# Seven pairs of up-projection tiles by one step of Strassen's scheme, in a hybrid decoder block on one core

## The chip, the cores and the metric

The kernel runs on one core of a Trainium2 chip. It computes one layer of a decoder for one sequence of 512 tokens, with 16 learned meta tokens ahead of them. The metric is the time of one execution on the device in microseconds (us). Five engines work side by side, each through its own queue in order: PE multiplies matrices (PEld is its weight load), DVE does elementwise work on one or two tensors, ACT does elementwise functions of one tensor, POOL is used here for little, and SP issues transfers from the main memory.

## The reference, cut to what matters

The layer normalises its input, projects it, mixes tokens in two ways, adds a projection of the mixed values, and ends in a gated part of which this is the whole:

```python
def rmsnorm(x, w):
    xf = x.astype(jnp.float32)
    y = xf * lax.rsqrt(jnp.mean(xf * xf, axis=-1, keepdims=True) + EPS)
    return (y * w.astype(jnp.float32)).astype(x.dtype)

def causal_dwconv(x, w, b):
    k_taps, length = w.shape[0], x.shape[1]
    xp = jnp.pad(x, ((0, 0), (k_taps - 1, 0), (0, 0)))
    y = b + xp[:, 0:length] * w[0]
    for k in range(1, k_taps):
        y = y + xp[:, k:k + length] * w[k]
    return y

def conv_glu_ffn(h, w_up, conv_w, conv_b, w_down):
    u = causal_dwconv(h @ w_up, conv_w, conv_b)
    gate, val = jnp.split(u, 2, axis=-1)
    return (jax.nn.silu(gate) * val) @ w_down
...
        h = h + conv_glu_ffn(rmsnorm(h, norm2_w[l]), ffn_w_up[l], ffn_conv_w[l],
                             ffn_conv_b[l], ffn_w_down[l])
    y = rmsnorm(h, final_norm_w)
    return y[:, N_META:, :]
```

The model is 1024 wide, the gated part 2816: `w_up` has 2 x 2816 columns, 22 tiles of 128 for the gate and 22 for the value. The convolution has three taps.

## The kernel before, in words

Channels lie on the 128 partitions, tokens along the free axis. A weight tile is 128 output channels by 1024 inputs (8 blocks k of 128). Every product in float32 quality is made of three faster ones: a weight tile `raw` is split into `whi` (ACT, L160) and `wlo` = raw - whi (DVE, L161), the tokens likewise into hi and lo, and for each k PE does whi x hi, whi x lo and wlo x hi. `product` (L190) does this for two halves of the tokens, which lie in two banks of PE's result memory: 8 x 3 x 2 = 48 matmuls for a tile, of 258 and 256 columns in the gated part.

The program runs in stages: input projection with both mixers (tiles `pj`), output projection (`pout`), the gated part's up-projection (`pup`), its down-projection (`pdn`), and a last normalisation. In the up stage pair j is the gate tile `pupj` and the value tile `pup(22+j)`: tile 24 is the value tile of pair 2. `conv3` (L790 and on) makes a tile: the product of `u2h`, `u2l` (tokens times the norm's weight, not yet divided by their size), then on DVE `fr` = pup x rstd2 (L797), which divides, on ACT the tap of the newest token with the bias (`fc`, L799), and on DVE two more taps (L801). After both tiles ACT does the silu, DVE the product (L810), and ACT and DVE split it into `ac_hi` and `ac_lo` (L813, L814) for the down stage. The reciprocal root `rstd2` exists only after the first tile, from `psn` (L785) through ACT (L130, L131).

Nothing of the order is written by hand. A scheduler puts the instructions of each engine in one list ahead of time, by priorities: weights come first (`first`), reading results out of PE's memory can be put higher still (`evac`). On the chip each engine follows its list and waits where an operand is not there or a buffer is not free. Buffers rotate: `pj` has two buffers of two banks for the tiles, `px` four of one bank, `raw`, `whi` and `wlo` three each, `pr` (for `fr` and `fc`) four. `weights` (L178 and on) asks for tiles two ahead, so a transfer into `raw` starts when the split of the tile three before it is done.

Of the kernel before, what the change touches and what calls it, by code (L numbers as in the profile page):

```python
# [29 lines left out]
O = 512 - HALF  # L30
# [24 lines left out]
def tile_block(ctx: ExitStack, tc: tile.TileContext, xT, w_in, w_dt, w_out, w_up, w_down,  # L55
               par, consts, consti, out, dbg=None):
    nc = tc.nc
    V, A, G, PE = nc.vector, nc.scalar, nc.gpsimd, nc.tensor

    cp = ctx.enter_context(tc.tile_pool(name="cp", bufs=1))  # L60
    wp = ctx.enter_context(tc.tile_pool(name="wp", bufs=3))
# [18 lines left out]
    def banks2(name):  # L80
        return pj.tile([P, 1024], F32, tag="pj", name=name)
# [13 lines left out]
    pt = cp.tile([P, C_ALL], F32, name="pt")  # L95
# [3 lines left out]
    def col(c):  # L99
        return pt[:, c:c + 1]  # L100
# [6 lines left out]
    with first(300000):  # L107
        w = A.activation(warm[:], eps[:], AF.Copy)
# [32 lines left out]
    chunks = [(("in", j), w_in[j], KD) for j in order]  # L141
# [9 lines left out]
    wnext = [0]  # L151

    def raw_tiles(key):
        name = "_".join(map(str, key))
        return (wp.tile([P, KD * P], F32, tag="raw", name=f"raw_{name}", bufs=3),
                wp.tile([P, KD * P], F32R, tag="whi", name=f"whi_{name}"),
                wp.tile([P, KD * P], F32R, tag="wlo", name=f"wlo_{name}"))

    def split_weights(raw, hi, lo, d, eng):
        A.activation(hi[:, d], raw[:, d], AF.Copy)  # L160
        eng.tensor_tensor(lo[:, d], raw[:, d], hi[:, d].bitcast(F32), ALU.subtract)  # L161

    def ahead(n):
        while wnext[0] < min(n, len(chunks)):
            key, src, kc = chunks[wnext[0]]
            with first():
# [9 lines left out]
    def weights(*key):  # L176
        used[0] += 1
        ahead(used[0] + 2)  # L178
        return wdone.pop(key)

    def product(groups, xh, xl, t0, nk, k0=0):


        for k in range(len(xh)):
            first, last = k0 + k == 0, k0 + k == nk - 1
            for ps, (hi, lo) in groups:
                wh, wl = hi[:, k * P:(k + 1) * P], lo[:, k * P:(k + 1) * P]
                for w, x, s, e in ((wh, xh[k], first, False), (wh, xl[k], False, False), (wl, xh[k], False, last)):
                    for a0, a1 in ((t0, HALF), (HALF, NT)):
                        PE.matmul(ps[:, O + a0:O + a1], w, x[:, a0:a1], start=s, stop=e)  # L190

    vh, vl, xt, sqs = [], [], [], []
    starts = [raw_tiles(("in", j)) for j in (BT, CT)]
    wnext[0] = 2
    with first(200000):
        for k in range(0, KD, 2):
            d = slice(k * P, (k + 2) * P)
            for j, w, kx in ((BT, starts[0], k), (CT, starts[1], k + 1)):  # L200
                t = slot(f"x{kx}", tag="y")
# [8 lines left out]
        for k in range(KD):  # L210
# [3 lines left out]
            tag = "b0" if k < 4 else "b1"  # L214
            hi, lo = slot(f"v{k}_hi", dtype=F32R, tag=tag), slot(f"v{k}_lo", dtype=F32R, tag=tag)
# [75 lines left out]
    for n, (a0, a1) in enumerate(((0, HALF), (HALF, NT))):  # L291
        p = bank(f"psd{n}")[0:66, :]
# [444 lines left out]
    for h in range(NH):  # L737
        o = os_[h]
        ps = proj(GT + h, T0)
        sg = slot(f"sg{h}", tag="pr")  # L740
# [3 lines left out]
        hi, lo = slot(f"oa{h}_hi", dtype=F32R), slot(f"oa{h}_lo", dtype=F32R)  # L744
# [7 lines left out]
    hs, u2h, u2l = [], [], []  # L752
    pos = {}
    acc = None
    for j, s in oorder:
        w = weights("out", j, s)
# [10 lines left out]
        hi, lo = slot(f"u2h{j}", dtype=F32R, tag="u"), slot(f"u2l{j}", dtype=F32R, tag="u")  # L767
# [22 lines left out]
    def conv3(j):  # L790
        w = weights("up", j)
        ps = banks2(f"pup{j}")
        product([(ps, w)], u2h, u2l, T0, KD)
        if j == 0:
            second_norm()
        r = slot(f"fr{j}", tag="pr")
        V.tensor_tensor(r[:, T0:], ps[:, O + T0:O + NT], rstd2[:, T0:], ALU.mult)  # L797
        c = slot(f"fc{j}", 512, tag="pr")
        A.activation(c[:], r[:, META:], AF.Identity, bias=col(C_FB + j), scale=col(C_FW + 88 + j))  # L799
        for s in (1, 2):  # L800
            V.scalar_tensor_tensor(c[:], r[:, META - s:NT - s], col(C_FW + (2 - s) * 44 + j), c[:],  # L801
                                   ALU.mult, ALU.add)
        return c

    ah, al = [], []
    for j in range(KF):
        c = conv3(j)
        silu = A.activation(c[:], c[:], AF.Silu)
        c2 = conv3(KF + j)
        V.tensor_tensor(c2[:], c2[:], c[:], ALU.mult)  # L810
        tag = ["b0"] * 4 + ["b1"] * 4 + ["m"] * 8 + ["ab"] * 2 + ["fqv"] * 2 + ["bc"] * 2
        hi, lo = slot(f"ac{j}_hi", 512, F32R, tag=tag[j]), slot(f"ac{j}_lo", 512, F32R, tag=tag[j])
        A.activation(hi[:], c2[:], AF.Copy)  # L813
        V.tensor_tensor(lo[:], c2[:], hi[:].bitcast(F32), ALU.subtract)  # L814
        ah.append(hi)
        al.append(lo)

# [13 lines left out]
    for j in range(KD):  # L831
# [3 lines left out]
        if j < KD - 1:  # L835
            ps = bank(f"pdn{j}")
# [7 lines left out]
        ps, halves = {}, (0, 256)  # L844
        for d0 in halves:
            d, dh = slice(d0, d0 + 256), slice(META + d0, META + d0 + 256)
            ps[d0] = bank(f"pdn{j}_{d0}")
            down(ps[d0][:, 0:256], ws, d)
        for d0 in halves:
            d, dh = slice(d0, d0 + 256), slice(META + d0, META + d0 + 256)  # L850
            with evac():
                V.tensor_tensor(hh[:, dh], hh[:, dh], ps[d0][:, 0:256], ALU.add)
                A.activation(sq[:, d], hh[:, dh], AF.Square)
                p = bank(f"psn3_{d0}")
                rs = slot(f"rs{d0}", 256, tag="u")
                if d0 == 0:
# [4 lines left out]
                    pr = rs  # L861
                else:

                    for b in range(2):
                        t = slice(d0 + b * P, d0 + (b + 1) * P)
# [6 lines left out]
                    pr = bank(f"psr3_{d0}")  # L872
# [81 lines left out]
```

## Time and profile before

| | |
|---|---|
| median of 3 runs | 893.63 us (893.51 to 894.04) |
| profiled execution | 893.47 us, span in the profile 891.3 us |
| PE busy | 871.7 us, 98% of the span, 6944 matmuls |
| DVE busy | 555.2 us, 62%, 873 instructions |
| ACT busy | 413.9 us, 46% |
| up stage (pup) | first matmul at 504.9 us, last at 756.9 us |

The span is the time from the first to the last instruction; the execution's own time is 2.2 us longer. Busy PE is counted from start to modelled end of overlapping matmuls, so the pace is better read as a window's length over its matmuls. A row of grouped instructions gives line, engine, operation, result <- operands, shape, count, then the sum of the busy time in us and the mean of one in ns, and last the idle time ahead of them with what ended it. In a row of the timeline stand start, length, engine, line and operation, and in brackets the idle time before it and what it waited for.

### The profile page before, as it was taken

How to read it: one execution, taken by the hardware profiler on the slowest of the kernel's cores; microseconds unless marked ns; L12 is line 12 of the kernel's file. 1: busy time of each engine (PE TensorE's matmuls, PEld its weight loads, DVE VectorE, ACT ScalarE, POOL GpSimd, SP SyncE). 2: the span in 40 equal slices, each digit the busy share in tenths (PEclk: the TensorE clock that was granted, in tenths of full speed). 3: DMA queues.
4: the chain of work that ended last, by engine and by line, in shares of the span. 5: the costliest groups of instructions: out<-in, count | busy, mean ns of one | idle time of the engine just before them, and what ended most of it. 6: DMA issues, size and time to landing. Idle time of an engine off the chain costs nothing.

```text
span 891.3 us, 16350 instructions
## 1 busy us (share of the span) xinstructions
PE 871.7 (98%) x6944; PEld 832.6 (93%) x6944; DVE 555.2 (62%) x873; ACT 413.9 (46%) x624; POOL 23.3 (3%) x46
## 2 busy tenths in 40 slices
PE   7999999999999999999999999999999999999995
PEld 7998899999999999999999999999999999888885
DVE  6975968698776767454333367776666667423333
ACT  8629955866446444353222364444444444323220
POOL 1000000010000000000000000000000000000001
PEclk9999999999999999999999999999999999999998
DMA  7234332212211322244223323222223333233312
GB/s 248 90 100 161 121 97 71 72 49 71 72 57 65 97 71 72 84 155 147 90 96 95 96 95 95 94 86 89 91 94 95 96 95 90 83 91 104 89 43 94
DMA packets 29081, 84.65 MB, mean 95 GB/s; under 512 B 3128, under 2 KB 6712, under 8 KB 29008
## 3 DMA queue, kind: packets, MB, share of 16 engines
q1 hardware_dynamic: 26480, 80.02, 28.5%
q10 hardware_dynamic: 2528, 3.60, 1.3%
q8 instruction: 54, 0.88, 0.4%
q14 instruction: 19, 0.16, 0.1%
HBM read 81.45 MB, written 2.15 MB: 94 GB/s over the span
## 4 chain that ended last, share of the span: by engine, by line
PE 83%; ACT 4%; DVE 4%; DMA 1%; issue 1%; SPq 0%; DVEq 0%; ACTq 0%
PE pup L190 28%; PE pj L190 24%; PE pout L190 10%; PE pdn L824 4%; PE pdn L823 4%; PE pdn L825 4%; ACT L L467 1%; PE psu L441 1%; PE po L704 1%; PE po L703 1%; PE pa L686 1%; PE pS L674 1%; DMA ab<-acum_d 1%; DMA rs_d<-rh 1%; PE psx L429 1%
## 5 line engine op out<-in xcount | busy, mean ns | idle before, releaser
L190 PE MATMUL pj<-u_hi,whi_in 128*128 128x272 f32 (+1 forms) x752 | 156.1, 287 | 2.3 <-ACT z L512 1.4
L190 PE MATMUL pj<-u_hi,wlo_in 128*128 128x272 f32 (+1 forms) x752 | 156.7, 287 | 0.0
L190 PE MATMUL pj<-u_lo,whi_in 128*128 128x272 f32 (+1 forms) x752 | 155.9, 286 | 0.0
L190 PE MATMUL pup<-u2h,wlo_up 128*128 128x258 f32 x704 | 141.6, 282 | 0.0
L190 PE MATMUL pup<-u2h,whi_up 128*128 128x258 f32 x704 | 140.7, 282 | 0.0
L190 PE MATMUL pup<-u2l,whi_up 128*128 128x258 f32 x704 | 140.6, 281 | 0.0
L190 PEld LDWEIGHTS pj<-u_hi,whi_in 128*128 128x128 f32 x752 | 115.7, 188 | 5.4 <-issue 2.5
L190 PEld LDWEIGHTS pj<-u_lo,whi_in 128*128 128x128 f32 x752 | 116.0, 188 | 2.0 <-issue 1.5
L190 PEld LDWEIGHTS pj<-u_hi,wlo_in 128*128 128x128 f32 x752 | 116.5, 189 | 1.3 <-issue 1.2
L190 PEld LDWEIGHTS pup<-u2h,wlo_up 128*128 128x128 f32 x704 | 108.0, 188 | 0.1
L190 PEld LDWEIGHTS pup<-u2l,whi_up 128*128 128x128 f32 x704 | 108.0, 189 | 0.0
L190 PEld LDWEIGHTS pup<-u2h,whi_up 128*128 128x128 f32 x704 | 107.6, 188 | 0.0
L161 DVE TENSOR_TENSOR wlo_in<-raw_in,whi_in 128x1024 fp32r<-128x1024 f32 (+1 forms) x58 | 64.3, 1108 | 54.2 <-ACT whi_in L160 53.8
L160 ACT ACTIVATE whi_in<-raw_in 128x1024 fp32r<-128x1024 f32 (+1 forms) x58 | 56.0, 966 | 54.3 <-PE pj L190 41.1
L825 PE MATMUL pdn<-ac_hi,wlo_dn 128*128 128x512 f32 (+1 forms) x198 | 73.0, 369 | 0.0
L823 PE MATMUL pdn<-ac_hi,whi_dn 128*128 128x512 f32 (+1 forms) x198 | 72.9, 368 | 0.0
L824 PE MATMUL pdn<-ac_lo,whi_dn 128*128 128x512 f32 (+1 forms) x198 | 72.9, 368 | 0.0
L160 ACT ACTIVATE whi_up<-raw_up 128x1024 fp32r<-128x1024 f32 x44 | 46.7, 1060 | 48.9 <-PE pup L190 32.4
L801 DVE SCALAR_TENSOR_TENSOR fc<-fr,pt,fc 128x512 f32<-128x512 f32 x88 | 65.9, 749 | 2.5 <-ACT fc L799 0.9
L161 DVE TENSOR_TENSOR wlo_up<-raw_up,whi_up 128x1024 fp32r<-128x1024 f32 x44 | 53.9, 1225 | 14.8 <-ACT whi_up L160 14.8
L161 DVE TENSOR_TENSOR wlo_dn<-raw_dn,whi_dn 128x1024 fp32r<-128x1024 f32 (+1 forms) x24 | 27.3, 1137 | 57.4 <-ACT whi_dn L160 57.4
L797 DVE TENSOR_TENSOR fr<-pup,rstd 128x514 f32<-128x514 f32 x44 | 30.5, 692 | 47.6 <-PE pup L190 43.5
(304 smaller groups left out, 1428.5 us busy)
## 6 DMA issues: line engine op xcount, KB each, us to landing
raw_in<-in_w_in_dram SPq DMA_DIRECT2D x50, 512.0 KB, 3.5
raw_up<-in_w_up_dram SPq DMA_DIRECT2D x44, 512.0 KB, 3.6
raw_out<-in_w_out_dram SPq DMA_DIRECT2D x16, 512.0 KB, 3.5
raw_dn<-in_w_down_dram SPq DMA_DIRECT2D x16, 512.0 KB, 3.5
ab<-acum_d SPq DMA_DIRECT2D x16, 264.0 KB, 4.7
raw_dn<-in_w_down_dram SPq DMA_DIRECT2D x8, 384.0 KB, 3.1
rb<-rs_d SPq DMA_DIRECT2D x8, 257.0 KB, 4.5
xr<-in_xT_dram ACTq DMA_DIRECT2D x8, 257.0 KB, 3.0
```

Of the source, the lines that this page charges most:

```text
L160: A.activation(hi[:, d], raw[:, d], AF.Copy)
L161: eng.tensor_tensor(lo[:, d], raw[:, d], hi[:, d].bitcast(F32), ALU.subtract)
L190: PE.matmul(ps[:, O + a0:O + a1], w, x[:, a0:a1], start=s, stop=e)
L429: PE.transpose(psx[0:n, t * P:(t + 1) * P], xs[t][:, a0:a1], ident)
L441: PE.matmul(psu[:], btk[0:n, b * P:(b + 1) * P], xdc[b][0:n, :], start=True, stop=True)
L467: A.activation(L[:, a0:a1], ab[:, a0:a1], AF.Relu, bias=acm[:, b, h:h + 1], scale=-1.0)
L674: PE.matmul(pS[:, b * P:(b + 1) * P], kt[:, (b - 1) * P:b * P], vt[:, (b - 1) * P:b * P], start=True, stop=True)
L797: V.tensor_tensor(r[:, T0:], ps[:, O + T0:O + NT], rstd2[:, T0:], ALU.mult)
L801: V.scalar_tensor_tensor(c[:], r[:, META - s:NT - s], col(C_FW + (2 - s) * 44 + j), c[:], ALU.mult, ALU.add)
L823: PE.matmul(ps, wh, xh, start=k0 + k == 0, stop=False)
L824: PE.matmul(ps, wh, xl, start=False, stop=False)
L825: PE.matmul(ps, wl, xh, start=False, stop=k0 + k == KF - 1)
```

## The change

The up stage gets three kinds of pairs, by the letters of `KINDS`: pairs 0 to 5 stay as they were (U). Pairs 6, 8, 10, 12, 14, 16, 18, 20 and 21 (N) use tokens `n` that are divided by their size once, so `fr` falls away and the taps read PE's result directly. Pairs 7, 9, ..., 19 (W, seven of them) are done as one 2 x 2 product of blocks: gate and value are the two block rows, the two halves of the 1024 inputs the blocks between, and two windows of 258 tokens (overlapping by two, for the taps) the block columns. `scheme` makes seven block products, p1, p2, p6 and two each in `p75` and `p43`, each of 4 k x 3 = 12 matmuls, 84 for a pair in place of 96. The sums of weight blocks (s1, s2, two sums in place) are made by DVE in `scheme_weights` and split again; the sums of results by DVE in `scheme`, where the value comes out negative, which `ntap` (taps times -1) undoes. `normed_tokens` makes the eight tiles n, their splits, and for four pairs of k the four sums of tokens t1 to t4 with their splits, once, after pair 0. Values `ac` are kept whole and split late: `ac_lo` of pairs 6 to 13 goes into the memory of the token sums, of pairs 14 to 21 into that of n.

```diff
@@
+KINDS = "UUUUUUNWNWNWNWNWNWNWNN"
+HT = 258
@@
+    def scheme_weights(key, src):
+        kind, j = key
+        if kind == "w0":
+            sums[j] = [raw_tile(key)]
+            nc.sync.dma_start(sums[j][0][:], src)
+            hi, lo = split_tiles(key)
+            split_weights(sums[j][0], hi, lo, slice(0, 2 * HK), V)
+            return hi, lo
+        if kind == "w2":
+            rg, rv = sums[j][0], raw_tile(key)
+            nc.sync.dma_start(rv[:], src)
+            s1, s2 = slot(f"s1_{j}", 512, tag="bc"), slot(f"s2_{j}", 512, tag="bc")
+            V.tensor_tensor(s1[:], rv[:, 0:HK], rv[:, HK:], ALU.add)
+            V.tensor_tensor(s2[:], s1[:], rg[:, 0:HK], ALU.add)
+            sums[j] += [rv, s2]
+            hi, lo = split_tiles(key)
+            split_half(s1[:], hi[:, 0:HK], lo[:, 0:HK])
+            split_half(s2[:], hi[:, HK:], lo[:, HK:])
+            return hi, lo
+        rg, rv, s2 = sums.pop(j)
+        V.tensor_tensor(rv[:, 0:HK], rv[:, 0:HK], rg[:, 0:HK], ALU.add)
+        V.tensor_tensor(rg[:, HK:], rg[:, HK:], s2[:], ALU.add)
+        hi, lo = split_tiles(key)
+        split_weights(rv, hi, lo, slice(0, 2 * HK), V)
+        h4, l4 = slot(f"s4h_{j}", 512, F32R, tag="ab"), slot(f"s4l_{j}", 512, F32R, tag="ab")
+        split_half(rg[:, HK:], h4[:], l4[:])
+        return hi, lo, h4, l4
@@
+    def normed_tokens():
+        for k in range(KD // 2):
+            f = []
+            for kk in (k, k + KD // 2):
+                t = slot(f"n{kk}", tag="z")
+                V.scalar_tensor_tensor(t[:, T0:], hs[kk][:, T0:], col(C_N2 + kk), rstd2[:, T0:], ALU.mult, ALU.mult)
+                tag = "b0" if kk % 4 < 2 else "b1"
+                hi, lo = slot(f"n{kk}_hi", dtype=F32R, tag=tag), slot(f"n{kk}_lo", dtype=F32R, tag=tag)
+                split_half(t[:, T0:], hi[:, T0:], lo[:, T0:])
...
+            V.tensor_tensor(t1, b11, b12, ALU.subtract)
+            V.scalar_tensor_tensor(t2, b22, -1.0, t1, ALU.mult, ALU.subtract)
+            V.tensor_tensor(t3, b22, b12, ALU.subtract)
+            V.scalar_tensor_tensor(t4, t2, -1.0, b21, ALU.mult, ALU.subtract)
+            ts.append([])
+            for n, t in enumerate((t1, t2, t3, t4)):
+                d = slot(f"t{n + 1}_{k}", 2 * HT, F32R)
+                split_half(t, d[:, 0:HT], d[:, HT:])
@@
+    def scheme(j):
+        p1, p2, p6 = (bank(f"p{n}_{j}")[:, 0:HT] for n in (1, 2, 6))
+        p75, p43 = banks2(f"p75_{j}"), banks2(f"p43_{j}")
...
+        hi, lo = weights("w0", j)
+        mul(p1, hi[:, 0:HK], lo[:, 0:HK], b11)
+        mul(p2, hi[:, HK:], lo[:, HK:], b21)
+        hi, lo = weights("w2", j)
+        mul(p6, hi[:, HK:], lo[:, HK:], t2)
+        mul(p75[:, 512:512 + HT], hi[:, 0:HK], lo[:, 0:HK], t1)
+        hi, lo, h4, l4 = weights("w1", j)
+        mul(p75[:, 0:HT], hi[:, 0:HK], lo[:, 0:HK], t3)
+        mul(p43[:, 512:512 + HT], h4, l4, b22)
+        mul(p43[:, 0:HT], hi[:, HK:], lo[:, HK:], t4)
+        with evac():
+            A.activation(sg[:, A_], p1, AF.Copy)
+            V.tensor_tensor(sv[:, A_], sg[:, A_], p6, ALU.add)
+            V.tensor_tensor(sg[:, A_], sg[:, A_], p2, ALU.add)
+            V.tensor_tensor(by_halves(su), sv[:, A_].unsqueeze(1).broadcast_to([P, 2, HT]), two(p75), ALU.add)
+            V.tensor_tensor(sv[:, B_], su[:, A_], p75[:, 512:512 + HT], ALU.add)
+            V.tensor_tensor(sv[:, A_], su[:, A_], p43[:, 0:HT], ALU.add)
+            V.tensor_tensor(sg[:, B_], su[:, B_], p43[:, 512:512 + HT], ALU.add)
@@
+        ac = slot(f"ac{j}", 512, tag="fqv" if j < 6 else "u")
+        V.tensor_tensor(ac[:], c2[:], c[:], ALU.mult)
+        acs.append(ac)
+        if j == 0:
+            normed_tokens()
     ah, al = [], []
+    tag = ["z"] * 2 + ["bc"] * 2 + ["ab"] * 2 + ["m"] * 8 + ["b0"] * 4 + ["b1"] * 4
+    for j, ac in enumerate(acs):
         hi, lo = slot(f"ac{j}_hi", 512, F32R, tag=tag[j]), slot(f"ac{j}_lo", 512, F32R, tag=tag[j])
+        split_half(ac[:], hi[:], lo[:])
```

What the scheduler makes of it stands in the engines' lists. The first place is DVE at the start of the up stage, from the first `fr` on, which needs rstd2. Before:

```order
L797 TENSOR_TENSOR fr0_5919<-pup0_5863,rstd2_5856 128x514
L801 SCALAR_TENSOR_TENSOR fc0_5921<-fr0_5919,pt_75,fc0_5921 128x512 x2
L797 TENSOR_TENSOR fr22_5981<-pup22_5932,rstd2_5856 128x514
L161 TENSOR_TENSOR wlo_up_2_5994<-raw_up_2_5992,whi_up_2_5993 128x1024
L801 SCALAR_TENSOR_TENSOR fc22_5983<-fr22_5981,pt_75,fc22_5983 128x512 x2
L810 TENSOR_TENSOR fc22_5983<-fc22_5983,fc0_5921 128x512
L797 TENSOR_TENSOR fr1_6047<-pup1_5998,rstd2_5856 128x514
```

Now, the same engine, the last rows ahead of `fr23` (the value tile of pair 1) and that row:

```order
L971 TENSOR_TENSOR ac0_5991<-fc22_5985,fc0_5923 128x512
L886 SCALAR_TENSOR_TENSOR fc1_6168<-fr1_6169,pt_75,fc1_6168 128x512
L173 TENSOR_TENSOR wlo_up_25_6302<-raw_up_25_6300,whi_up_25_6301 128x1024
L870 SCALAR_TENSOR_TENSOR t24_2_6066<-t24_2_6066,n6_6059 128x258
L180 TENSOR_TENSOR t2_2_6074<-t24_2_6066,t2_2_6074 128x258
L869 TENSOR_TENSOR t13_3_6095<-n7_6089,n3_6083 128x258
L180 TENSOR_TENSOR t3_2_6077<-t13_2_6065,t3_2_6077 128x258
L180 TENSOR_TENSOR n7_lo_6092<-n7_6089,n7_hi_6091 128x514
L868 SCALAR_TENSOR_TENSOR t24_3_6096<-n7_6089,t13_3_6095 128x258
L905 TENSOR_TENSOR fr23_6231<-pup23_6181,rstd2_5856 128x514
```

From `fr0` to `fr23`, both counted, DVE's list before has 14 instructions. Now it has 56: 4 `fr`, 8 n (128x514), their 8 `n_lo` (128x514), 8 sums t1 or t3 and 7 sums t2 or t4 (128x258), 11 low parts of such sums (128x258), 5 taps `fc`, 4 `wlo` and 1 `ac`. `fr23` frees the buffer that tile 24 is multiplied into.

The second place is DVE in an ordinary W pair, here pair 11. `sv` (first row) reads p6, the last row's `sv` reads `p75` for the last time and so frees its buffer for the next tile, `pup12`. Between them now stand weight work for the next tiles and the first sum of pair 13's weights:

```order
L950 TENSOR_TENSOR sv11_7389<-sg11_7388,p6_11_7385 128x258
L951 TENSOR_TENSOR sg11_7388<-sg11_7388,p2_11_7384 128x258
L173 TENSOR_TENSOR wlo_up_34_7459<-raw_up_34_7457,whi_up_34_7458 128x1024
L952 TENSOR_TENSOR su11_7390<-sv11_7389,p75_11_7386 128x516
L196 TENSOR_TENSOR s1_13_7577<-raw_w2_13_7575 128x512
L953 TENSOR_TENSOR sv11_7389<-su11_7390,p75_11_7386 128x258
```

Ahead of these, from the last matmul of the pair before on, DVE's list has `wlo_w1_11`, two taps of `fc32`, `wlo_up_12` and `ac10`. The buffer of `raw_w2_13`, which `s1_13` reads, is the one that `wlo_up_12` empties.

The third place is the same stretch in the last W pair, 19, where there is no further W pair to prepare:

```order
L950 TENSOR_TENSOR sv19_8425<-sg19_8424,p6_19_8421 128x258
L180 TENSOR_TENSOR ac6_lo_8818<-ac6_6863,ac6_hi_8817 128x512
L180 TENSOR_TENSOR ac7_lo_8822<-ac7_6995,ac7_hi_8821 128x512
L180 TENSOR_TENSOR ac8_lo_8826<-ac8_7122,ac8_hi_8825 128x512
L951 TENSOR_TENSOR sg19_8424<-sg19_8424,p2_19_8420 128x258
L173 TENSOR_TENSOR wlo_up_42_8495<-raw_up_42_8493,whi_up_42_8494 128x1024
L952 TENSOR_TENSOR su19_8426<-sv19_8425,p75_19_8422 128x516
L180 TENSOR_TENSOR ac9_lo_8830<-ac9_7254,ac9_hi_8829 128x512
L180 TENSOR_TENSOR ac10_lo_8834<-ac10_7381,ac10_hi_8833 128x512
...
L180 TENSOR_TENSOR ac13_lo_8846<-ac13_7772,ac13_hi_8845 128x512
L953 TENSOR_TENSOR sv19_8425<-su19_8426,p75_19_8422 128x258
```

Nine low parts of gated values (pairs 5 to 13) stand between the `sv` that reads p6 and the `sv` that frees `p75`; three of the nine are left out above. On PE the tiles follow each other as the loops are written; its list is 84 matmuls shorter. SP's list has as many transfers as before, in the same order of tiles.

More of the change, by code (lines that the diff above doesn't have):

```diff
@@ L151, in tile_block, with raw_tile, split_tiles @@
     wnext = [0]
+    def raw_tile(key):
+        return wp.tile([P, KD * P], F32, tag="raw", name="raw_" + "_".join(map(str, key)), bufs=3)
+    def split_tiles(key):
+        name = "_".join(map(str, key))
+        return (wp.tile([P, KD * P], F32R, tag="whi", name=f"whi_{name}"),
+                wp.tile([P, KD * P], F32R, tag="wlo", name=f"wlo_{name}"))
     def raw_tiles(key):
[L154 to L157, printed above, removed]
+        return (raw_tile(key),) + split_tiles(key)
     def split_weights(raw, hi, lo, d, eng):
@@ L165, in ahead @@
             key, src, kc = chunks[wnext[0]]
+            if key[0] in ("w0", "w1", "w2"):
+                with first():
+                    wdone[key] = scheme_weights(key, src)
+                wnext[0] += 1
+                continue
             with first():
@@ L787, in second_norm @@
         log_exp(rstd2, parts, T0, 1.0 / DM)
-    def conv3(j):
+    ntap = cp.tile([P, 3 * KF], F32, name="ntap")
+    for i in range(3):
+        V.tensor_scalar(ntap[:, i * KF:(i + 1) * KF], pt[:, C_FW + i * 2 * KF + KF:C_FW + (i + 1) * 2 * KF],
+                        -1.0, None, ALU.mult)
+    tails = (slice(T0, T0 + HT), slice(NT - HT, NT))
+    nh, nl, ts = [None] * KD, [None] * KD, []
+    def normed_tokens():
[7 more added lines that the diff above has]
+                split_half(t[:, T0:], hi[:, T0:], lo[:, T0:])
+                nh[kk], nl[kk] = hi, lo
+                f += [t[:, c] for c in tails]
+            b11, b12, b21, b22 = f
+            t13, t24 = slot(f"t13_{k}", tag="ab"), slot(f"t24_{k}", tag="ab")
+            t1, t3, t2, t4 = t13[:, 0:HT], t13[:, HT:2 * HT], t24[:, 0:HT], t24[:, HT:2 * HT]
+            V.tensor_tensor(t1, b11, b12, ALU.subtract)
[6 more added lines that the diff above has]
+                split_half(t, d[:, 0:HT], d[:, HT:])
+                ts[-1].append((d[:, 0:HT], d[:, HT:]))
@@ L791, in conv3, with taps, at, taps_of @@
+    def taps(c, r, j, w, b):
+        n = c.shape[-1]
+        def at(s):
+            return r[..., 2 - s:2 - s + n] if len(r.shape) == 2 else r[:, :, 2 - s:2 - s + n]
+        A.activation(c, at(0), AF.Identity, bias=b, scale=w[2])
+        for s in (1, 2):
+            V.scalar_tensor_tensor(c, at(s), w[2 - s], c, ALU.mult, ALU.add)
+    def taps_of(j):
+        return [col(C_FW + i * 2 * KF + j) for i in range(3)]
+    def conv3(j, kind):
         w = weights("up", j)
         ps = banks2(f"pup{j}")
-        product([(ps, w)], u2h, u2l, T0, KD)
+        if kind == "U":
+            product([(ps, w)], u2h, u2l, T0, KD)
+        else:
+            product([(ps, w)], nh, nl, T0, KD)
@@ L794, in conv3 @@
         if j == 0:
             second_norm()
-        r = slot(f"fr{j}", tag="pr")
-        V.tensor_tensor(r[:, T0:], ps[:, O + T0:O + NT], rstd2[:, T0:], ALU.mult)
+        r = ps[:, O + T0:O + NT]
         c = slot(f"fc{j}", 512, tag="pr")
[L799 to L802, printed above, removed]
@@ L803, in conv3 @@
-        return c
-    ah, al = [], []
[L806 to L811, printed above, removed]
+        with evac():
+            if kind == "U":
+                t = slot(f"fr{j}", tag="pr")
+                V.tensor_tensor(t[:, T0:], r, rstd2[:, T0:], ALU.mult)
+                r = t[:, T0:]
+            taps(c[:], r, j, taps_of(j), col(C_FB + j))
@@ new lines, in tile_block @@
+    acs = []
+    for j in range(KF):
+        if KINDS[j] == "W":
+            c, c2 = scheme(j)
+            silu = A.activation(c[:], c[:], AF.Silu)
+        else:
+            c = conv3(j, KINDS[j])
+            silu = A.activation(c[:], c[:], AF.Silu)
+            c2 = conv3(KF + j, KINDS[j])
+        ac = slot(f"ac{j}", 512, tag="fqv" if j < 6 else "u")
[3 more added lines that the diff above has]
+            normed_tokens()
+    ah, al = [], []
```

35 lines of the change are left out of this document (32 added, 3 removed).

## The prediction

> **What bounds the kernel now.** First the page, then windows of the up stage, then the tile `pup` with who waits for it.
>
> ```profile
> span 891.3 us, 16350 instructions
> PE 871.7 (98%) x6944; PEld 832.6 (93%) x6944; DVE 555.2 (62%) x873; ACT 413.9 (46%) x624; POOL 23.3 (3%) x46
> 600.00:650.00 50.00, 50.00 (x423) 50.00 (x422) 35.56 (x46) 21.91 (x27) 0.00 (x0) 1.00 0.31 96
> 800.00:850.00 50.00, 50.00 (x218) 40.63 (x217) 16.14 (x18) 14.39 (x17) 0.00 (x0) 1.00 0.34 98
> 512.25 244.93 PE pup L190 x2060
>   DVE fr L797: 43.5, 21
>   ACT whi_up L160: 32.4, 36
> ```
>
> The third row is 50 us of the up stage: PE 50.00 us busy with 423 matmuls, so 0.1182 us each, DVE 35.56 us, ACT 21.91. The chain that ended last runs 244.93 us on PE there in one piece. DVE and ACT wait for PE (last two rows: 43.5 and 32.4 us), not the other way. So a matmul removed here is worth its 0.1182 us, as long as DVE, busy 71% of the time, keeps out of the way. How far that holds decides this case.
>
> **What is removed.** Seven pairs lose 12 matmuls each: 84 x 0.1182 = 9.93 us. The 588 that stay in these pairs are 258 columns wide, where half had 256, so one column more on average. From the fourth row a 512-column matmul paces at 50/218 = 0.2294, so a column is (0.2294 - 0.1182)/255 = 0.44 ns, together 0.3 us. That all 12 matmuls of a product go into one bank costs nothing more, as the last tile of the down stage shows, which does that too (0.12 us apart):
>
> ```profile
> 868.38 0.28 PE L823 MATMUL pdn<-ac_hi,whi_dn 128*128 128x256 f32 x1
> 868.50 0.28 PE L824 MATMUL pdn<-ac_lo,whi_dn 128*128 128x256 f32 x1
> ```
>
> Net gain 9.6 us. The `fr` of 32 tiles goes too, but on DVE, which gives no time by itself.
>
> **What is added at the start of the stage.** The token work of `normed_tokens` can't begin before rstd2, and DVE's list puts nearly all of it ahead of `fr23`. The durations it needs, and DVE's timeline of before at that place:
>
> ```profile
> L801 DVE SCALAR_TENSOR_TENSOR fc<-fr,pt,fc 128x512 f32<-128x512 f32 x88 | 65.9, 749 | 2.5 <-ACT fc L799 0.9
> L161 DVE TENSOR_TENSOR wlo_up<-raw_up,whi_up 128x1024 fp32r<-128x1024 f32 x44 | 53.9, 1225 | 14.8 <-ACT whi_up L160 14.8
> L814 DVE TENSOR_TENSOR ac_lo<-fc,ac_hi 128x512 fp32r<-128x512 f32 x22 | 15.2, 692 | 14.7 <-ACT ac_hi L813 14.6
> L651 DVE TENSOR_TENSOR kBC<-k,sd 128x256 f32<-128x256 f32 x8 | 3.3, 417 | 0.0
> L881 DVE SCALAR_TENSOR_TENSOR ot<-xr,pt,rs 128x256 f32<-128x256 f32 x1 | 0.5, 471 | 0.0
> 516.18 0.69 DVE L797 TENSOR_TENSOR fr<-pup,rstd 128x514 f32<-128x514 f32 x1 [2.88 <-ACT rstd L131]
> 522.09 1.53 DVE L801 SCALAR_TENSOR_TENSOR fc<-fr,pt,fc 128x512 f32<-128x512 f32 x2
> 523.65 0.69 DVE L810 TENSOR_TENSOR fc<-fc,fc 128x512 f32<-128x512 f32 x1
> 524.26 0.68 DVE L797 TENSOR_TENSOR fr<-pup,rstd 128x514 f32<-128x514 f32 x1
> 528.95 0.69 DVE L797 TENSOR_TENSOR fr<-pup,rstd 128x514 f32<-128x514 f32 x1 [0.28 <-PE pup L190]
> 540.36 0.69 DVE L797 TENSOR_TENSOR fr<-pup,rstd 128x514 f32<-128x514 f32 x1 [1.90 <-PE pup L190]
> ```
>
> The 56 instructions from `fr0` to `fr23`: 21 of two tensors and 514 columns at 0.692 (4 `fr`, 8 `n_lo`, `ac0`: 13 = 9.00 us), 13 with a scalar at 0.749 (8 n, 5 taps: 9.74), 19 of 258 at 0.417 (7.92), 7 with a scalar at 0.471 (3.30), 4 `wlo` at 1.225 (4.90): 34.9 us. Independent instructions overlap: at 523.65 and 524.26 the second starts 0.61 after the first, 0.08 before its end. None of the 56 needs the one right before it, so 55 x 0.08 = 4.4 comes off: 30.5. `fr0` starts at 516.18 as before (nothing ahead of it changed), `fr23` ends at 546.7. Only then may PE start tile 24, since its buffer is the one `fr23` reads.
>
> Before, tile 24 was the one whose `fr` waited for PE until 540.36. It ended at about 540.2, and its 48 matmuls take 5.7, so it began at about 534.5. The stall is 546.7 - 534.5 = **12.2 us**. I see it fall into pieces: `fr22` is the 12th instruction (7.2 us after 516.18) and holds up tile 23 by 0.3; `fr1` is the 27th (ends near 531.3) and holds up tile 2 by another 2; the rest, 9.7 us, is one gap between tiles 2 and 24, from 537.0 to 546.7. Bounds: 16.6 if nothing overlaps, 11 if each instruction overlaps by 0.1. I take the overlap that the rows show. ACT has 24 copies more there (8 of 514 columns, 16 of 258) and was half idle, so it is not late. After `fr23` stand 3.8 us of DVE work up to `fr2`, less than a tile of PE: the stall ends there.
>
> **What the gap does to PE's clock.** The start of the kernel, after 5.95 us without work, and the windows at its end:
>
> ```profile
> 5.95 0.81 PE L190 MATMUL pj_b<-v_hi,whi_in 128*128 128x272 f32 x2 [5.95 <-ACT v_hi L216]
> 11.40 0.55 PE L190 MATMUL pj_b<-v_hi,whi_in 128*128 128x272 f32 x2
> 11.79 0.41 PE L190 MATMUL pj_c<-v_hi,whi_in 128*128 128x272 f32 x2
> 13.02 0.40 PE L190 MATMUL pj_b<-v_hi,whi_in 128*128 128x272 f32 x2
> 884.00:886.00 2.00, 0.46 (x4) 0.27 (x3) 1.09 (x4) 0.38 (x1) 1.04 (x2) 0.88 0.00 0
> 886.00:888.00 2.00, 0.00 (x0) 0.00 (x0) 1.05 (x3) 0.00 (x0) 0.38 (x1) 0.50 0.70 230
> ```
>
> 24 matmuls take from 5.95 to 11.40, 0.227 each, and then 10 from 11.79 to 13.02, 0.123 each. And when PE runs out of work at the end, the granted clock falls to 0.50 within about 2 us. So tile 24 should begin at half pace: 24 x 0.104 = **2.5 us** lost. Bounds 0 and 5. The gap of the last W pair (below) is too short to be sure of; I count nothing there.
>
> The Trainium skill (TensorE: Matmul & The Clock Gate, HAM oscillation) says that PE-idle gaps over about 3.4 us put the clock back to half, and that as long a busy stretch restores it. By it the loss after such a gap would be near 1.7 us, as an estimate, once or twice. The trace agrees with the fall (0.50) and shows a longer return (5.45 us).
>
> **What is added in the last W pair.** Count from E, the end of tile 40. PE has seven products before tile 20: 84 x 0.1182 = 9.93. Tile 20 needs `p75` free. DVE can start `wlo_w1_19` only when ACT has made its `whi` (1.06, from E on): E + 1.2. From it to the freeing `sv` stand 19 instructions: 3 of 1024 columns (3.68), two taps in a row (1.53), `ac18` and `su` and the nine `ac_lo` (11 x 0.692 = 7.61), three of 258 (1.25): 14.1, less 17 x 0.08: 12.7. So p75 is free at E + 13.9, with some 0.1 of hand-over; PE waits **4.1 us**. Bounds 3.5 and 5.5. Without the nine `ac_lo` it would not.
>
> ```profile
> L160 ACT ACTIVATE whi_up<-raw_up 128x1024 fp32r<-128x1024 f32 x44 | 46.7, 1060 | 48.9 <-PE pup L190 32.4 <-PE pout L190 9.3 <-issue 7.2
> raw_up<-in_w_up_dram SPq DMA_DIRECT2D x44, 512.0 KB, 3.6
> DMA to landing us min/median/max: 3.4/3.6/4.5
> ```
>
> **The six other W pairs.** DVE's own row there is short of E + 9.93: 8.5 us from E + 1.2, less overlaps, is E + 9.0. But `s1` of the next W pair stands ahead of the freeing `sv` and needs a transfer: p2's end at 2.84, `whi_up` 1.06, `wlo_up` 1.23, landing 3.6, `s1` 0.69, `sv` 0.42 and four hand-overs of 0.04 make E + 10.0. That is level with PE. With the slowest landing of before, 4.5, PE would wait 0.9. Two loads come 3 us apart now, so I take 0.2 each, **1.2 us** for six; bounds 0 and 5.4. Over a whole W and N period DVE has 4 instructions of 1024 columns, 10 of 512, 5 of 258 and 8 taps, 4.90 + 6.92 + 2.09 + 5.99 = 19.9 us, against 180 x 0.1182 = 21.3 of PE: tight, but not the bound.
>
> **At nothing.** Three tiny `ntap` instructions at the kernel's start hide behind PE's half-pace first matmuls (0.5 if not). The late splits of pairs 14 to 21 (8 x 0.61 on DVE) hide behind the first 14 k of the down stage (42 x 0.2294 = 9.6); without that cover, 5. SP's list has the same transfers.
>
> **Sum.** 893.47 - 9.9 + 0.3 + 12.2 + 2.5 + 4.1 + 1.2 = 903.9. The median is 0.16 above the profiled execution: **904 us**, 1.2% slower.
>
> **The rivals.**
> - *DVE keeps pace and PE is never held at the start* (faster). Then 12.2 and 2.5 go: 889. It decides from the point where the 56 take under about 22.5 us, 0.40 each: then stall, 4.1 and 1.2 together fall below 9.6. For it: DVE work with one tensor is quicker per column. Against it: nearly all 56 read two tensors, and those rows have 0.417 for 256 columns and 0.69 for 512 wherever they stand.
> - *Nothing overlaps*, because nearly every instruction now has a wait of its own: +4.4 at the start, +1.4 in the last W pair: 910. Against it: the `fr` at 524.26 waits for PE, long done, and overlaps.
> - *The load for `s1` lands late in every W pair*: six times 0.7 more, 908. For it: loads closer together; against it: DMA's share is 0.31.
> - *The clock does not fall*: 901.5, inside the forecast's own range.
>
> The Trainium skill (VectorE: DVE Perf Modes, The DRAIN you can't avoid) states that the next operation waits until the pipeline is empty, unless it is one that isn't held. Its first half would give the second rival; the rows above show the second half.
>
> **How the numbers follow.** Forecast 0.70, nothing overlaps 0.10, late loads 0.10, DVE keeps pace 0.08, the remainder (a smaller stall that just cancels) 0.02. Bounds taken together on the low side: 893.5 - 9.6 + 11 + 0 + 3.5 + 0 = 898.4. On the high side all bounds at once would give 916, which is not likely; 911 takes in either slower rival. Range 898 to 911. A measurement of this kernel can tell about 0.2%. Faster 0.08, same 0.02, slower 0.90.
>
> **What would show it.** 6860 matmuls; PE idle once for near 10 us between 537 and 547, ended by DVE `fr`, with DVE solid from 516; a granted clock under 1 right after; PE idle for near 4 us at about 740, ended by a DVE `sv`; the other six W pairs with gaps under 1 us. The forecast is wrong if DVE is through with `fr23` before 540, if PE has no gap there, or if the W pairs each show gaps of some us.

## The result, and the profile after

The changed kernel takes 905.22 us, median of 4 runs (904.01 to 906.74), and the kernel before, run beside it, 893.84 (893.51 to 894.4). The ratio is 1.0123, 95% interval 1.011 to 1.0135: slower by 1.2%. The forecast was 904. The profiled execution is the quickest of the four: 904.01 us, with a span of 902.2. Below are its span and its first engine row from the page, then two rows of PE's table of waits (engine, waiting line, releasing line: us in total, times, longest).

```profile
span 902.2 us, 16342 instructions
PE 866.9 (96%) x6860; PEld 826.5 (92%) x6860; DVE 593.1 (66%) x983; ACT 432.8 (48%) x676; POOL 23.3 (3%) x46
```

```profile
PE pup L244 <- DVE fr L905: 11.1, 3, 9.2
PE pup L244 <- DVE sv L953: 3.9, 1, 3.9
```

PE has the 84 matmuls less that were to go (6944 to 6860), and its busy time fell by 4.8 us (871.7 to 866.9), not by 9.6. Two rows are new, and both name DVE: 11.1 us behind `fr` and 3.9 behind `sv`. No other W pair is in the table. The timelines of DVE and PE at the start of the stage and in the last W pair show where these waits stand:

```profile
516.16 0.69 DVE L905 TENSOR_TENSOR fr<-pup,rstd 128x514 f32<-128x514 f32 x1 [2.88 <-ACT rstd L135]
522.57 0.69 DVE L905 TENSOR_TENSOR fr<-pup,rstd 128x514 f32<-128x514 f32 x1
530.26 0.69 DVE L905 TENSOR_TENSOR fr<-pup,rstd 128x514 f32<-128x514 f32 x1
545.34 0.70 DVE L905 TENSOR_TENSOR fr<-pup,rstd 128x514 f32<-128x514 f32 x1
...
734.95 1.89 DVE L180 TENSOR_TENSOR ac_lo<-ac,ac_hi 128x512 fp32r<-128x512 f32 x3
...
738.83 3.70 DVE L180 TENSOR_TENSOR ac_lo<-ac,ac_hi 128x512 fp32r<-128x512 f32 x6
742.44 0.42 DVE L953 TENSOR_TENSOR sv<-su,p 128x258 f32<-128x258 f32 x1
```

```profile
523.41 0.47 PE L244 MATMUL pup<-u2h,whi_up 128*128 128x258 f32 x2 [0.24 <-DVE fr L905]
531.11 0.47 PE L244 MATMUL pup<-u2h,whi_up 128*128 128x258 f32 x2 [1.74 <-DVE fr L905]
546.18 0.77 PE L244 MATMUL pup<-u2h,whi_up 128*128 128x258 f32 x2 [9.16 <-DVE fr L905]
743.00 0.47 PE L244 MATMUL pup<-n_hi,whi_up 128*128 128x258 f32 x2 [3.88 <-DVE sv L953]
```

The four `fr` are those of tiles 0, 22, 1 and 23. From the start of the first to the end of the last are 29.9 us, in which DVE never pauses. PE's gaps of 0.24, 1.74 and 9.16 us end 0.14 to 0.16 us behind `fr22`, `fr1` and `fr23`. In the last W pair nine `ac_lo` stand ahead of the `sv` that frees `p75`. After both large gaps PE is slow for a while, as its windows show (the last two are cut where the clock changes; us; PE busy and matmuls; weight loads; DVE; ACT; POOL; granted clock; DMA share; GB/s):

```profile
540.00:545.00 5.00, 0.00 (x0) 0.00 (x0) 5.00 (x11) 1.36 (x3) 0.00 (x0) 0.50 0.30 105
545.00:550.00 5.00, 3.81 (x19) 3.85 (x20) 5.00 (x12) 2.37 (x5) 0.00 (x0) 0.54 0.18 74
740.70:744.11 3.41, 1.10 (x9) 1.14 (x10) 3.41 (x8) 0.55 (x1) 0.00 (x0) 1.00 0.21 80
744.11:747.52 3.41, 3.41 (x18) 3.41 (x17) 3.31 (x6) 1.60 (x3) 0.00 (x0) 0.50 0.50 141
```

A window's count takes in the matmuls that are already running at its start. Counted by their starts there are 421 in 50 us of undisturbed up stage, so the full pace is 0.1189 us each. The 19 matmuls of the second row, all started in it, would take 2.26 us at that pace, so 1.6 are lost there. In the last row 16 start (two of its 18 were running before), which would take 1.9 of the 3.41 us, so another 1.5 are lost.

### The profile page after: what moved, and what is told of

Read it like the earlier page. It is cut to its first block, busy times and chain, and to the rows that moved or that the text cites. A ratio compares the mean times of both kernels' runs of the same rounds, so it can differ in the third digit from the quotient of the medians.

```text
span 902.2 us, 16342 instructions
## 1 busy us (share of the span) xinstructions
PE 866.9 (96%) x6860; PEld 826.5 (92%) x6860; DVE 593.1 (66%) x983; ACT 432.8 (48%) x676; POOL 23.3 (3%) x46
## 4 chain that ended last, share of the span: by engine, by line
PE 79%; DVE 6%; ACT 4%; issue 2%; DMA 1%; SPq 0%; DVEq 0%; ACTq 0%
PE pj L244 24%; PE pup L244 17%; PE pout L244 10%; PE pdn L990 4%; PE pdn L989 4%; PE pdn L988 4%; PE p L924 3%; PE p L923 3%; PE p L925 3%; ACT L L521 1%; PE psu L495 1%; PE po L758 1%; PE po L757 1%; PE pa L740 1%; DMA rs_d<-rh 1%
## 5 line engine op out<-in xcount | busy, mean ns | idle before, releaser
L244 PE MATMUL pup<-n_hi,whi_up 128*128 128x258 f32 (+1 forms) x288 | 58.7, 285 | 3.9 <-DVE sv L953 3.9
L172 ACT ACTIVATE whi_dn<-raw_dn 128x1024 fp32r<-128x1024 f32 (+1 forms) x24 | 23.7, 989 | 78.7 <-PE pdn L989 67.9
L244 PE MATMUL pup<-n_hi,wlo_up 128*128 128x258 f32 (+1 forms) x288 | 58.3, 284 | 0.0
L244 PE MATMUL pup<-n_lo,whi_up 128*128 128x258 f32 (+1 forms) x288 | 58.3, 284 | 0.0
L172 ACT ACTIVATE whi_up<-raw_up 128x1024 fp32r<-128x1024 f32 x30 | 31.8, 1059 | 52.4 <-PE pup L244 18.1
L244 PE MATMUL pup<-u2h,whi_up 128*128 128x258 f32 x192 | 39.2, 287 | 11.1 <-DVE fr L905 11.1
L244 PEld LDWEIGHTS pup<-n_hi,whi_up 128*128 128x128 f32 x288 | 44.7, 191 | 4.4 <-issue 4.3
L173 DVE TENSOR_TENSOR wlo_up<-raw_up,whi_up 128x1024 fp32r<-128x1024 f32 x30 | 36.8, 1225 | 15.0 <-ACT whi_up L172 15.0
L244 PEld LDWEIGHTS pup<-n_hi,wlo_up 128*128 128x128 f32 x288 | 44.8, 191 | 0.0
L244 PEld LDWEIGHTS pup<-n_lo,whi_up 128*128 128x128 f32 x288 | 44.7, 190 | 0.0
```

## The experiments

The theory has three parts: the start stalls because of the order of DVE's list, not because of the amount of its work; the gap costs its own length and a stretch at half clock behind it; and the W pairs are a real gain that both stalls cover. Each run is compared with the kernel before on the same chip: the first four ran on one chip, the last four on another, and the kernel before takes 894.0 us on both.

### Spread the token work

```diff
-        if j == 0:
-            normed_tokens()
...
+    UNITS = [2] * 12
...
+    def some_tokens(x):
+        if tile_no[0] < len(UNITS):
+            with tc.issue_after(x.ins):
+                for _ in range(UNITS[tile_no[0]]):
+                    next(tokens, None)
+        tile_no[0] += 1
...
-            taps(c[:], r, j, taps_of(j), col(C_FB + j))
+            x = taps(c[:], r, j, taps_of(j), col(C_FB + j))
+        some_tokens(x)
```

`normed_tokens` hands out its work here in 24 pieces (8 of one n, 16 of one sum with its split); two are queued on DVE behind the last tap of each of the first twelve tiles.

> The same token work, cut into 24 pieces (8 of one n with its split, 16 of one sum with its split), two of them queued on DVE behind the last tap of each of the first twelve tiles. Theory A (the place in DVE's order): the three waits for `fr` at the start, 11.1 us in the changed kernel, go, and with them about 1.5 us of half-pace matmuls; the 3.9 us wait in the last W pair stays. Profiled execution 904.0 - 12.6 = 891.4, ratio to the kernel before 0.998. Theory B (the amount: DVE has no room for some 21 us more beside the first six pairs): gaps of 0.5 to 1 us at many tiles, 6 to 10 us in all, 899 to 903.

Measured: 892.8 us (891.09 to 894.11), ratio 0.9987 (0.9977 to 0.9996), 12.4 us below the changed kernel. No wait for `fr` is left in the table of waits, and the one for `sv` stands. Two of its windows where the changed kernel stalls, then its row for `sv`:

```profile
530.00:535.00 5.00, 5.00 (x44) 5.00 (x44) 4.98 (x10) 3.13 (x5) 0.00 (x0) 1.00 0.42 119
545.00:550.00 5.00, 5.00 (x44) 5.00 (x43) 5.00 (x10) 2.42 (x4) 0.00 (x0) 1.00 0.29 105
```

```profile
PE pup L244 <- DVE sv L972: 4.1, 2, 3.9
```

DVE is as full from 530 to 550 as in the changed kernel (4.98 and 5.00 of 5 us in the two rows), yet PE is never held. So the order made the stall; the amount of the work, of which nothing was taken away, did not.

### Put the late splits behind the last W pair

```diff
-        split_half(ac[:], hi[:], lo[:])
+        with tc.issue_after(last.ins) if j >= 8 else contextlib.nullcontext():
+            split_half(ac[:], hi[:], lo[:])
```

Here `last` is the `sg` that ends the evacuation of W pair 19; the token work stays where the change put it.

> The changed kernel, but 14 of the 22 late splits of gated values (those of pairs 8 to 21) are queued on DVE behind the last evacuation of the last W pair; eight stay free. Theory A (the splits ahead of the freeing `sv` make the wait): the 3.9 us wait in the last W pair falls to 0.6 or less, the 1.2 us of slow clock after it goes too, and the down stage gives none of it back: 904.0 - 4.5 = 899.5, ratio 1.0065. Theory B (the moved splits are late at the down stage): a new wait of PE for `ac_lo` of 2 to 4 us, and the time stays at 902 to 904.

Measured: 899.99 us (899.45 to 900.64), ratio 1.0072 (1.0057 to 1.0088), 5.2 us below the changed kernel. The waits of PE:

```profile
PE pup L245 <- DVE fr L906: 11.1, 3, 9.1
PE pup L245 <- DVE sv L954: 0.8, 2, 0.6
```

The start is the same to a tenth. Of the nine splits between the two `sv` of the last W pair six are queued later here and three still stand there. The wait in that place shrank from 3.9 to 0.27 us; the 0.6 of the row is at an earlier W pair, until 653.56. From 738 to 746 the clock stays at 1.00, and no wait for an `ac_lo` came instead. The late splits were the cause, and the down stage hides them.

### Both edits

The two diffs above together, with nothing else changed.

> Both edits: token work spread over the first twelve tiles, and 14 late splits behind the last W pair. Theory A: the two stalls are separate and all that is wrong with the change, so both gains add: 904.0 - 12.6 - 4.5 = 886.9, ratio 0.9925, faster than the kernel before. Theory B (they share cover: the work moved out of the start makes the W pairs late): 890 to 895, with waits over 1 us in other W pairs.

Measured: 885.83 us (885.36 to 887.1), ratio 0.9916 (0.9899 to 0.9933). This kernel beats both the changed one (by 19.4 us) and the kernel before (by 0.8%). The gains alone are 12.4 and 5.2, so together they bring 1.8 us more than their sum. Part of that may be the clock: in the profiled execution of the run with the work spread, the gap at the last W pair lost 2.3 us behind it and not 1.5 (last section). The rest isn't explained.

```profile
PE 863.8 (98%) x6860; PEld 823.8 (93%) x6860; DVE 591.7 (67%) x983; ACT 431.1 (49%) x676; POOL 23.3 (3%) x46
```

```profile
PE pup L245 <- DVE sv L973: 0.5, 2, 0.3
```

PE does the same 6860 matmuls in 3.1 us less busy time than in the changed kernel (866.9), which is the 1.6 + 1.5 us lost at half clock that the changed kernel's windows show.

### Fill the gap

```diff
+        if j == KF + 2:
+            with tc.issue_after(last_mm[0].ins):
+                d = bank("fill")
+                for n in range(72):
+                    PE.matmul(d[:, 0:258], w[0][:, 0:P], u2h[0][:, T0:T0 + 258], start=True, stop=True)
```

> The changed kernel with 72 more matmuls of 258 columns (8.5 us of PE at full pace) behind tile 2, in the gap before tile 24; they write a bank that nobody reads, so the kernel does more work than the reference needs. The stall itself stays, since DVE is as late as before. Theory A (the idle gap puts the clock down, and the half-pace matmuls behind it are a cost of their own): tile 24 starts at 546.2 as before, but its first matmuls pace at 0.118 and not at 0.215, granted clock 1.00 at 545 to 550: 904.0 - 1.5 = 902.5. Theory B (the first matmuls are slow for another reason, weights or DVE traffic): they stay at 0.215 and the time at 904.

Measured: 902.81 us (901.88 to 903.45), ratio 1.0103 (1.0088 to 1.0118): 2.4 us below the changed kernel, though the two intervals overlap a little. The trace decides. First tile 24 in PE's timeline, then the windows about it:

```profile
546.44 0.47 PE L246 MATMUL pup<-u2h,whi_up 128*128 128x258 f32 x2 [0.55 <-DVE fr L912]
546.75 0.40 PE L246 MATMUL pup<-u2l,whi_up 128*128 128x258 f32 x2
546.98 0.40 PE L246 MATMUL pup<-u2h,wlo_up 128*128 128x258 f32 x2
```

```profile
540.00:545.00 5.00, 5.00 (x44) 5.00 (x43) 5.00 (x11) 1.41 (x4) 0.00 (x0) 1.00 0.33 93
545.00:550.00 5.00, 4.45 (x38) 4.28 (x37) 5.00 (x12) 2.38 (x5) 0.00 (x0) 1.00 0.24 91
```

The tile starts 0.26 us later than in the changed kernel, at full pace: two matmuls start 0.23 us after the two ahead of them, where it took 0.43 in the changed kernel:

```profile
546.75 0.63 PE L244 MATMUL pup<-u2l,whi_up 128*128 128x258 f32 x2
547.18 0.63 PE L244 MATMUL pup<-u2h,wlo_up 128*128 128x258 f32 x2
```

Same weights, same DVE traffic, other pace: the idle gap alone slows what follows. The profiled execution gains only 0.6 us in all (903.41 against 904.01), in part because its second gap cost more: half clock from 741.52 to 747.44, 27 matmuls, 2.7 us lost where the changed kernel lost 1.5.

### No W pairs, with the block at the start, without the sums, and spread

Three kernels without W pairs price the parts apart. The first has only this edit:

```diff
-KINDS = "UUUUUUNWNWNWNWNWNWNWNN"
+KINDS = "UUUUUUNNNNNNNNNNNNNNNN"
```

> The changed kernel with all token work, its sums too, but no W pair: pairs 6 to 21 are of kind N, so the sums are computed and not used. Theory A (the W pairs are a gain of 1.3 us each against an N pair, 11.44 to 10.12 by the trace of the changed kernel, and the start is a loss): the start stands as in the changed kernel, 11.1 us of waits and 1.5 of slow clock, the N pairs cost 0.09 more than U pairs each: 893.6 + 12.6 + 0.4 + 1.4 = 908.0, ratio 1.016, slower than the changed kernel by 4 (9.2 of W pairs less 3.9 and 1.2 of their last stall). Theory B (the W pairs are no gain on the chip): 904 or less.

Measured: 907.73 us (907.38 to 908.23), ratio 1.0151 (1.0134 to 1.0168). The waits for `fr` are again 11.1 us, with 9.14 in one. The kernel is 2.5 us slower than the one with W pairs (3.4 by the profiled executions), where 4 was expected.

The second leaves the sums out as well:

```diff
-            b11, b12, b21, b22 = f
-            t13, t24 = slot(f"t13_{k}", tag="ab"), slot(f"t24_{k}", tag="ab")
...
-                ts[-1].append((d[:, 0:HT], d[:, HT:]))
```

> As the one before, and the token sums t1 to t4 with their splits are left out (nothing uses them without W pairs): 32 DVE instructions fewer, of which 26 stood ahead of `fr23`. Theory A (the stall follows the number of instructions ahead of `fr23`): 19 x 0.34 + 7 x 0.39 = 9.2 us earlier, so the waits for `fr` fall from 11.1 to about 2.2, and with no gap over 2 us the clock stays at 1.00: 893.6 + 2.2 + 0.4 + 1.4 = 897.6, ratio 1.0045. Theory B (the stall comes from the n tensors alone, the sums hide): 905 or more.

Measured: 895.87 us (895.43 to 897.54), ratio 1.0022 (1.0012 to 1.0031).

Its row for `fr`, and the window behind that wait:

```profile
PE pup L244 <- DVE fr L893: 1.7, 1, 1.7
```

```profile
535.00:540.00 5.00, 4.17 (x35) 4.20 (x36) 4.96 (x8) 2.32 (x4) 0.00 (x0) 1.00 0.41 134
```

With 32 DVE instructions fewer, 9.4 us of the wait are gone, and the clock stays at 1.00. The stall follows what stands ahead of `fr23`. The time is 1.7 us under the 897.6 expected; that sum held 1.4 for slower N pairs, which the next kernel doesn't show.

The third has the first one's `KINDS` and the spread token work of the first experiment.

> The token work spread as in the run with both edits, but pairs 6 to 21 of kind N, the sums unused. It prices the W pairs with no stall in the way. Theory A: 893.6 + 1.4 (N pairs at 11.44) + 0.4 = 895.4, ratio 1.002, so that seven W pairs are worth 9 to 9.6 us against the run with both edits. Theory B (the slower pace belongs to the W pairs only): 893.6, ratio 1.000.

Measured: 894.11 us (893.36 to 895.91), ratio 0.9999 (0.999 to 1.0009). So theory B was right on the N pairs: alone they run like U pairs, 423 matmuls in 50 us.

```profile
600.00:650.00 50.00, 50.00 (x423) 50.00 (x422) 29.63 (x37) 20.31 (x26) 0.00 (x0) 1.00 0.31 96
```

It also shows that all of the token work can be had for nothing, and it prices the W pairs: against the kernel with both edits, 894.11 - 885.83 = 8.3 us for seven, 1.2 each. And it prices the start: against the kernel with the block and no W pairs, 907.73 - 894.11 = 13.6 us.

### Ten W pairs

```diff
-KINDS = "UUUUUUNWNWNWNWNWNWNWNN"
+KINDS = "UUUUUUNWWNWWNWWNWWNWWN"
```

This on top of both edits, with the splits from pair 10 on queued late.

> Both edits with ten W pairs, not seven: from pair 7 on W, W, N five times, 12 of the late splits behind the last W pair. DVE needs some 31 us per W, W, N by its rows, PE 2 x 10.12 + 11.44 = 31.7. Theory A (the amount decides, so it still fits): three more W pairs bring 1.32 each: 885.8 - 4 = 882. Theory B (the order decides: after two W pairs in a row the evacuation of one stands behind the weights of the next, and PE waits 1 to 2.4 us at each): 889 to 893, with waits of PE for DVE in every such group.

Measured: 895.3 us (891.58 to 897.27), ratio 1.0015 (1.0 to 1.003), 9.5 us worse than with seven. The waits of PE that are new against the run with both edits:

```profile
PE p L943 <- ACT whi_w L173: 4.3, 4, 1.1
PE pup L245 <- DVE sv L973: 2.0, 1, 2.0
PE p L945 <- DVE wlo_w L174: 1.6, 2, 0.8
PE pdn L1007 <- ACT whi_dn L173: 1.1, 1, 1.1
```

From 585 to 740 us DVE is busy for 138.0 of 155 us, so the amount of DVE work doesn't decide here either. The loss is above what theory B gave (889 to 893), and by another road. The four rows are 9.0 us. Behind three of the waits the clock is at 0.50 for 3.41 us each (from 641.24, 709.51 and 747.05), some 1.5 us lost each time. With 3 x 1.2 for the three further W pairs that makes, as an estimate, 9.0 - 0.5 + 4.5 - 3.6 = 9.4 us against the run with both edits, close to the 9.5 measured. Most of the waiting is for a W pair's first weights, not for an evacuation: at one of the four places ACT makes `whi_w` only after 3.21 us without work that PE's product before it ended.

```profile
706.73 1.06 ACT L173 ACTIVATE whi_w<-raw_w 128x1024 fp32r<-128x1024 f32 x1 [3.21 <-PE p L944]
707.84 0.39 PE L943 MATMUL p<-n_hi,whi_w 128*128 128x258 f32 x1 [1.03 <-ACT whi_w L173]
```

That points to the weight buffers. A kernel with more of them was not tried, so that stays open.

## Why the prediction was right

The sum was right to 1.2 us of 905.2, and its two stalls came at their places, by their releasers and at their sizes. Term by term:

- **The removed matmuls.** Predicted 9.6. The two kernels without stalls (spread, with and without W pairs) give 8.3 by medians. By their profiled executions it is 894.43 - 886.02 = 8.4, and 0.5 of the shortfall is the rest of the wait for `sv`. The pace of 0.1182 was read a little low, from a count that takes in the matmuls already running: in the kernel before, 96 matmuls take 11.41 us (585.82 to 597.23), 0.1189 each. The mis-sized term is the pace in the W pairs, where I allowed 0.3 us for all 588. The first W pair of the changed kernel takes 10.17 us (599.15 to 609.32) for 84, so 0.121 each, where 84 x 0.1189 and its share of the 0.3 make 10.03. The six without a wait in the table take 10.10 to 10.29, 0.7 us too long together. On average they take 10.15: 11.41 - 10.15 = 1.26 each, 8.8 in seven, and less 0.5 of waits that is the 8.3. The rows, two of the kernel before and three of the changed one:

```profile
585.82 0.40 PE L190 MATMUL pup<-u2h,whi_up 128*128 128x258 f32 x2
597.23 0.40 PE L190 MATMUL pup<-u2h,whi_up 128*128 128x258 f32 x2
```

```profile
599.15 0.28 PE L923 MATMUL p<-n_hi,whi_w 128*128 128x258 f32 x1
609.32 0.47 PE L244 MATMUL pup<-n_hi,whi_up 128*128 128x258 f32 x2
620.81 0.28 PE L923 MATMUL p<-n_hi,whi_w 128*128 128x258 f32 x1
```

The N pair behind it takes 11.49, and the others between W pairs 11.42 to 11.50, so a little of the slower pace is theirs too; it can't all be the 258 columns. What makes it wasn't tested.

- **The start.** Predicted 12.2, measured 11.1. The pieces came as drawn: 0.24, 1.74 and 9.16 for 0.3, 2 and 9.7. The block took 29.9 us for 30.5, so independent instructions overlap by (34.9 - 29.9)/55 = 0.09 and not 0.08 each. (The list of the 56 in the prediction says 21 where 13 are added up; its sum is right.) The step held because it counted DVE's list up to the one instruction that PE waits for. The runs with the work spread and with the sums left out both confirm it.
- **The clock behind that gap.** Predicted 2.5 from the kernel's start, measured 1.6 in the changed kernel's windows. The fill shows that it is the gap's doing. The size was taken from the return at the kernel's start, which is slower (5.45 us, against the 3.4 or so here). The prediction's other estimate, near 1.7 from the Trainium skill (TensorE: Matmul & The Clock Gate, HAM oscillation), was the better one, and its "once or twice" came true as twice.
- **The last W pair.** Predicted 4.1, measured 3.9, and with six of the nine `ac_lo` queued later 0.27 was left in that place. But "too short to be sure of; I count nothing there" was wrong: the clock fell there too, for 1.5 us more.
- **The six other W pairs.** Predicted 1.2, measured about 0.2 in all: only the last W pair has a wait for `sv` in the table. In two of the six DVE waits for the load of `s1`, 0.15 and 0.28 us, and PE goes on to the next tile 0.17 and 0.31 us after the start of the pair's last matmul, where the other four take 0.12.
- **At nothing.** The late splits hide behind the down stage, as the kernel that moved 14 of them later shows. The kernel without W pairs and with the work spread stands at 0.9999, so the token work and the `ntap` cost nothing that can be measured.

Errors of both signs met, so part of the agreement is luck. The gain was 1.2 too high and the second clock loss was left out at 1.5. The start was 1.1 too high, its clock 0.9, and the six W pairs 1.0. From the profiled execution with both edits, the measured terms give 886.02 + 11.1 + 1.6 + 3.4 + 1.5 = 903.6 (3.4 being the 3.9 less the 0.5 of waits that both edits leave), and the profiled execution of the changed kernel took 904.0; 0.4 us are not accounted for.

Of the rivals, "DVE keeps pace" is refuted for the order that the change has, and true as soon as the order is mended. "Nothing overlaps" is refuted by the 29.9, "late loads" by the table of waits, and "the clock does not fall" by the windows.

## What to carry to other kernels

Added work on an engine that is two thirds busy is free or holds up the bounding engine, depending on where it stands in that engine's list (here the same token work cost 11.1 us of waits as a block and none when spread): count what stands ahead of each instruction that frees a buffer of the bounding engine. Pace such work explicitly, some pieces behind each tile, and queue work that nobody needs yet behind the evacuation that somebody waits for. A gap on TensorE of some us has a second price, here 1.5 to 2.7 us lost at half clock behind it, and two short waits close together can have it too.

## What the runs showed of the hardware that was not expected

The clock falls late. After the 3.88 us gap of the changed kernel PE starts at full pace and slows only 1 us later:

```profile
743.55 0.40 PE L244 MATMUL pup<-n_hi,wlo_up 128*128 128x258 f32 x2
743.79 0.40 PE L244 MATMUL pup<-n_hi,whi_up 128*128 128x258 f32 x2
744.38 0.63 PE L244 MATMUL pup<-n_hi,wlo_up 128*128 128x258 f32 x2
744.81 0.63 PE L244 MATMUL pup<-n_hi,whi_up 128*128 128x258 f32 x2
```

With ten W pairs two waits of 1.03 and 0.82 us, four matmuls apart, were enough to halve it, while a wait of 1.07 us alone left it at 1.00 (PE's timeline of that kernel, then its windows about the single wait, about the two, and behind them):

```profile
674.95 0.39 PE L943 MATMUL p<-n_hi,whi_w 128*128 128x258 f32 x1 [1.07 <-ACT whi_w L173]
709.40 0.50 PE L945 MATMUL p<-n_hi,wlo_w 128*128 128x258 f32 x1 [0.82 <-DVE wlo_w L174]
```

```profile
671.96:675.38 3.42, 2.35 (x19) 2.14 (x19) 3.42 (x7) 1.55 (x2) 0.00 (x0) 1.00 0.45 132
706.10:709.51 3.41, 1.57 (x11) 1.15 (x11) 3.41 (x6) 1.58 (x2) 0.00 (x0) 1.00 0.60 183
709.51:712.92 3.41, 3.41 (x16) 3.41 (x17) 3.41 (x8) 1.92 (x3) 0.00 (x0) 0.50 0.00 0
```

These windows are cut at the times at which the clock can change. In every trace of this case the stretches between two changes of the clock last whole multiples of 3.41 us. Cut the same way, the up stages of all the runs show one line: the clock fell at the end of a window in which PE was busy for 1.57 us or less (the second row; 46%), and did not where it was busy for 1.67 us or more (49%; the changed kernel, 529.07 to 532.48, with its wait of 1.74). So about half a window of idle time decides here, in one piece or in two. The two short waits, 1.85 us of idle time within 2.6, lay in one window; the single one left 2.35 us busy. The clock came back only after a window that was busy for at least 3.37 us; in the fill 2.50 us busy, from 740.61 to 744.02, did not bring it back.

The late fall goes with that. The changed kernel's 3.88 us gap filled 1.6 us of one window and 2.3 of the next, which ended at 744.11, after the gap. It also makes the loss vary: the kernel with the token work spread has the same gap, until 731.29, but its clock fell in the middle of it, at 729.58, and the next window was half idle too. So PE ran at 0.50 from 731.29 to 736.41, 24 matmuls with 2.3 us lost, where the changed kernel lost 1.5.

```profile
731.29 0.77 PE L244 MATMUL pup<-n_hi,whi_up 128*128 128x258 f32 x2 [3.88 <-DVE sv L972]
729.58:736.41 6.83, 5.12 (x24) 5.15 (x25) 6.71 (x12) 2.15 (x3) 0.00 (x0) 0.50 0.30 82
```

The Trainium skill (TensorE: Matmul & The Clock Gate, What's actually happening) says that a monitor watches how busy TensorE was in a free-running window of about 3.4 us, and that the transition point depends on where in the window the first matmul lands. The traces agree, with the steps of 3.41 us. The Trainium skill's table in that section speaks of at least one idle window for the fall; here a window that was idle for 54% was enough, so the measurement says more.
